# One-hots of a gate table with two tokens innermost in place of four, and the gate product as two instructions

## The chip, the cores and the metric

The kernel runs on one core of a Trainium2 chip. A core has a matrix engine (TensorE, PE in the profile, with the loading of its weights shown apart as PEld), three engines for elementwise work (VectorE or DVE, ScalarE or ACT, GpSimd or POOL), and a queue engine that here only starts transfers (SyncE or SP). They run their own instruction streams and wait for each other by semaphores. Operands lie in SBUF, matmul results in PSUM, in banks of 512 floats per partition. The metric is the device time of one execution in microseconds (us), the median of several. Before the change it is 2301.12 us, with three runs from 2299.87 to 2302.93.

## The reference

The reference is one layer of a decoder block over 256 tokens of width 2048: a combined projection, two kinds of attention, a merge with an output projection and a layer norm, then a PEER layer (a retrieval over 16,384 one-neuron experts) and a second layer norm. The change lies in the PEER layer, which computes, cut to its core:

```python
q = (yc @ w_q).reshape(PEER_CHUNK, PEER_HEADS, 2, half)
s1 = jnp.einsum('chd,nd->chn', q[:, :, 0], sub_k1)
s2 = jnp.einsum('chd,nd->chn', q[:, :, 1], sub_k2)
v1, i1 = lax.top_k(s1, PEER_TOPK)          # 16 of 128 keys, 8 heads
v2, i2 = lax.top_k(s2, PEER_TOPK)
...                                        # the best 16 of the 16 x 16 pairs
eid = jnp.take_along_axis(cid, j, axis=-1) # expert = 128 * key1 + key2
gate = jax.nn.softmax(sc, axis=-1)
act = jax.nn.gelu(jnp.einsum('chkd,cd->chk', u_tab[eid], yc))
return jnp.einsum('chk,chkd->cd', gate * act, v_tab[eid])
```

Each token thus has 8 x 16 = 128 slots, and a slot has a first key, a second key (both 0 to 127) and a gate.

## The kernel before

**The dense form.** Nothing is gathered. The kernel multiplies all 16,384 rows of u with the tokens (the U product), applies gelu, multiplies by a table G that holds for every expert and token the sum of the gates of that token's slots, and multiplies the result with all of v (the V product). u and v are streamed once from memory in pieces of 128 x 1024 floats.

**Exact products from two parts.** Each streamed piece `raw` is split into `hi` (a copy rounded by ScalarE, line 96) and `lo` (the rest, a subtraction on VectorE, line 97). A product of two such operands is three matmuls: hi with hi, hi with lo, lo with hi. All matmuls go through the helper `mm`, so most have line 189 in the profile, and they are told apart by their tiles. In the U product a matmul has 128 x 128 of u as weights and streams the 256 tokens of `yhi` or `ylo` into a bank `acc`.

**The gate table G.** For one token, G as a 128 x 128 table (first key by second key) is a sum over the token's 128 slots of one-hot(first key) times one-hot(second key) times gate. With the slots on the partitions that is one matmul. The transposed slots lie in `slotT`, 2-byte numbers, one row of 256 tokens per kind: first key, second key, and the gate in two parts (lines 1126 to 1128). For four tokens (a block q, 64 blocks in all) `g_onehot` makes on VectorE:

- `one`, the one-hots of both keys: a ramp `keys` of the 128 key numbers, each repeated for the four tokens, compared with the slots' keys (line 1189), 2 x 128 x 4 elements with the tokens innermost;
- `ob`, the one-hot of the second key times both parts of the gate (line 1190), again 2 x 128 x 4.

`g_mm` then takes for each of the four tokens the column k of `one` as weights and of `ob` as streamed operand, once for each part of the gate: 8 matmuls of 128 columns into a bank `lg`. The operands of one token are 128 elements of 2 bytes with a step of 4 elements. The deferred part of the block scales the four tables: part of the first half of G on VectorE, multiplied with gelu results already in G (line 1205), the rest on ScalarE (lines 1208, 1209).

**Order.** The order is the order of the code; there is no scheduler. `step` handles one streamed piece: it runs the deferred work, takes background work from a list `slots` as far as a credit goes (one credit a step; a block costs 1.05), splits the pieces for the next two steps (`W.ahead`, depth 2), issues the step's 24 U matmuls, and behind these the background work's matmuls. So in a step VectorE gets: line 1205 of the block whose matmuls ended the step before, then `one` and `ob` of a new block, then two subtractions of line 97 for the step after the next; and TensorE gets 24 U matmuls and the 8 matmuls of the block whose one-hots were made one step earlier. Every fourth step ScalarE also applies gelu to a finished bank (line 1241) and, while G is not ready, spills it to memory from its own queue (line 1245). `one` and `ob` have three buffers each, `lg` two banks. Transfers of u are started on SP (line 77) as soon as one of three `raw` buffers is free.

Of the kernel before, what the change touches and what calls it, by code (L numbers as in the profile page):

```python
# [11 lines left out]
F16 = mybir.dt.float16  # L12
# [3 lines left out]
AF = mybir.ActivationFunctionType  # L16
OP = mybir.AluOpType
# [4 lines left out]
S = 256  # L22
# [10 lines left out]
GSCALE = 2.0 ** 14  # L33
# [95 lines left out]
def block_kernel(ctx, tc, x, xT, w_in, rel_bias, onehot, lamq, lamk, subln_g, pe, w1, w2k, w2v, cmask,  # L129
                 wbda, wbnsa, wout, ln1_gT, ln1_bT, ln1_g, ln1_b, wq, subk, u, v, ln2_g, ln2_b, out):  # L130
    nc = tc.nc
    V, A, PE, GP = nc.vector, nc.scalar, nc.tensor, nc.gpsimd
# [52 lines left out]
    def bank(name, bufs):  # L185
        return ps.tile([128, 512], F32, name=name, bufs=bufs)

    def mm(o, a, b, start, stop):
        PE.matmul(o, a, b, start=start, stop=stop, skip_group_check=True)  # L189
# [679 lines left out]
    for q in range(2):  # L869
        for t in range(2):  # L870
            c = slice(HALF * q, HALF * q + HALF)
# [54 lines left out]
    yp = pY.enter_context(tc.tile_pool(name="yp", bufs=1, side="right"))  # L926
# [52 lines left out]
    pH.close()  # L979
    pX.close()  # L980
    pT = ExitStack()
    slotT = yp.tile([128, 4, S], F16, name="slotT")
    tk = pT.enter_context(tc.tile_pool(name="tk", bufs=1, side="right"))
    gb = lp.tile([128, 2, D], F32, name="gd")

# [33 lines left out]
    def h_rows():  # L1019
        for t in range(2):  # L1020
            for n in range(4):
                c = slice(n * 512, n * 512 + 512)
                d = r1[:, t, c]
                GP.tensor_tensor(d, d, gb[:, 0, c], op=OP.mult)
                GP.tensor_tensor(d, d, gb[:, 1, c], op=OP.add)
            GP.dma_start(h_d[:, t, :], r1[:, t, :])
# [92 lines left out]
    def sel_T(t):  # L1119
        tp = bank("tp", 1)  # L1120
        for c in range(3):
            PE.transpose(tp[:, 128 * c:128 * c + 128], sel[:, c, t, :], ident_k)

        def ev():
            ts = slice(128 * t, 128 * t + 128)
            A.copy(slotT[:, 0:2, ts], tp[:, 0:256].rearrange("p (c s) -> p c s", c=2))
            A.activation(slotT[:, 2, ts], tp[:, 256:384], AF.Copy, scale=GSCALE)
            V.scalar_tensor_tensor(slotT[:, 3, ts], tp[:, 256:384], GSCALE, slotT[:, 2, ts],
                                   op0=OP.mult, op1=OP.subtract)
        deferred.append(ev)  # L1130

    gs = {"done": False}
# [5 lines left out]
    def open_G(i):  # L1138
        if i == 0:
            h_rows()  # L1140
            pL.close()
        else:
            pT.close()
            gs["oh"] = pO.enter_context(tc.tile_pool(name="ohp", bufs=1, side="right"))
            gs["n0"] = len(stashed)
            keys = gs["keys"] = gs["oh"].tile([128, 128, 4], F16, name="keys")
            GP.iota(keys, pattern=[[1, 128], [0, 4]], base=0, channel_multiplier=0,
                    allow_small_or_imprecise_dtypes=True)
        gp = pG[i].enter_context(tc.tile_pool(name=f"gp{i}", bufs=1))
        gs["G", i] = gp.tile([128, HI, S], F32, name=f"G{i}")  # L1150

    bg(0.5, lambda: open_G(0))
    for c in range(2):
        if c == 0:
# [28 lines left out]

    def g_onehot(q):

        shape = [128, 2, 128, 4]
        one, ob = [gs["oh"].tile(shape, F16, name=x, bufs=3) for x in ("one", "ob")]
        key12, gate12 = [slotT[:, c:c + 2, None, 4 * q:4 * q + 4].to_broadcast(shape) for c in (0, 2)]
        V.tensor_tensor(one, gs["keys"][:, None, :, :].to_broadcast(shape), key12, op=OP.is_equal)
        V.tensor_tensor(ob, one[:, 1:2].to_broadcast(shape), gate12, op=OP.mult)  # L1190
        gs[q] = (one[:, 0], ob)

    def g_mm(q):
        gps = bank("lg", 2)
        oa, ob = gs.pop(q)
        for k in range(4):
            for c in range(2):
                mm(gps[:, 128 * k:128 * k + 128], oa[:, :, k], ob[:, c, :, k], k == 0 and c == 0, c == 1)

        def ev():  # L1200
            gv = gps.rearrange("p (t i) -> p i t", t=4)
            ts = slice(4 * q, 4 * q + 4)
            n0 = min(2 * gs["n0"], HI)
            g0, g1 = gs["G", 0], gs["G", 1]
            V.scalar_tensor_tensor(g0[:, 0:n0, ts], gv[:, 0:n0, :], 1.0 / GSCALE, g0[:, 0:n0, ts],
                                   op0=OP.mult, op1=OP.mult)
            if n0 < HI:
                A.activation(g0[:, n0:HI, ts], gv[:, n0:HI, :], AF.Copy, scale=1.0 / GSCALE)
            A.activation(g1[:, :, ts], gv[:, HI:I2, :], AF.Copy, scale=1.0 / GSCALE)
            if q == 63:  # L1210
                gs["done"] = True
                pO.close()
        deferred.append(ev)

    bg(0.1, lambda: open_G(1))
    for q in range(65):
        bg(GCOST, lambda q=q: g_onehot(q) if q < 64 else None, lambda q=q: g_mm(q - 1) if q else None)
# [270 lines left out]
```

## Time and profile before

| what | value |
|---|---|
| median of three runs | 2301.12 us |
| profiled execution, by the clock around it | 2305.7 us |
| its span, first to last instruction | 2303.9 us |
| TensorE busy | 2271.5 us (99%) |
| VectorE busy | 1436.8 us (62%) |
| ScalarE busy | 1116.7 us (48%) |
| stretch with the 64 gate blocks | 988.3 to 1236.1 us |
| granted TensorE clock, mean | 0.996 |

The busy shares are averages over the whole span. A timeline row gives the start, the time from the first start to the last end of a run of like instructions, the engine, the line, the operation with its tiles (output <- inputs), the shape, the count, and in brackets how long the engine sat idle before it and what ended that. Matmuls are pipelined: the time that one takes is longer than the time from its start to the next one's, and it is the second that counts. The pace of a run of n matmuls is its time less the length of one, over n - 1.

### The profile page before, as it was taken

What the parts mean: (1) busy time and instruction counts of PE and PEld (TensorE: products, weight loads), DVE (VectorE), ACT (ScalarE), POOL (GpSimd) and SP (SyncE); (2) the same over time, 40 slices, a digit from 0 to 9 for tenths busy, and PEclk for the clock granted to TensorE, in tenths of its full rate; (3) what the DMA queues carried; (4) which work ended last, traced back from release to release, by engine and by line L of the source; (5) the groups of instructions that cost most, each with busy time, mean ns of one, the idle gap of its engine ahead of it and who ended that gap; (6) DMA issues with size and microseconds to landing.
All of it is one profiled execution on the core that took longest, in us unless ns stands there. A gap on an engine that the chain in (4) does not pass through costs nothing.

```text
span 2303.9 us, 40869 instructions
## 1 busy us (share of the span) xinstructions
PE 2271.5 (99%) x15712; PEld 2084.5 (90%) x15712; DVE 1436.8 (62%) x2834; ACT 1116.7 (48%) x2153; POOL 245.8 (11%) x223
## 2 busy tenths in 40 slices
PE   9999999999999999999999999999999999999997
PEld 9989999999987999999999999998888888888786
DVE  5458664665657989977776555555555555555557
ACT  4455654665545544454444444444444444444443
POOL 1002234442002402200000000000000000000002
PEclk9999999999999999999999999999999999999999
DMA  7554564545575655554545666666666656667764
GB/s 241 185 182 150 177 188 138 156 143 174 184 234 174 221 181 173 181 173 158 159 157 174 184 187 188 187 188 198 190 187 188 189 187 190 185 191 234 243 210 145
DMA packets 119844, 424.73 MB, mean 184 GB/s; under 512 B 13876, under 2 KB 14212, under 8 KB 119392
## 3 DMA queue, kind: packets, MB, share of 16 engines
q1 hardware_dynamic: 111600, 398.90, 55.4%
q0 software_dynamic: 5600, 18.75, 2.7%
q10 hardware_dynamic: 2448, 4.46, 0.5%
q8 instruction: 123, 2.02, 0.3%
q14 instruction: 73, 0.60, 0.1%
HBM read 413.37 MB, written 8.69 MB: 183 GB/s over the span
## 4 chain that ended last, share of the span: by engine, by line
PE 86%; DVE 6%; DMA 4%; ACT 2%; issue 1%; POOL 0%; DVEq 0%; ACTq 0%; SPq 0%; POOLq 0%
PE acc L189 53%; PE o L189 27%; PE lg L189 4%; DVE lo L97 3%; DMA raw<-in_v_dram 2%; PE pv L189 1%; DMA raw<-in_wq_dram 1%; DMA raw<-in_wout_dram 1%; PE tp L527 1%; DMA raw<-in_w_in_dram 1%; ACT hi L96 1%; DVE eq L1095 0%; DVE st L890 0%; DVE r L922 0%; DVE eid L1099 0%
## 5 line engine op out<-in xcount | busy, mean ns | idle before, releaser
L97 DVE TENSOR_TENSOR lo<-raw,hi 128x512 fp32r<-128x512 f32 (+1 forms) x1422 | 969.4, 718 | 595.6 <-ACT hi L96 593.5
L96 ACT CAST hi<-raw 128x512 fp32r<-128x512 f32 (+1 forms) x1494 | 859.4, 615 | 730.0 <-PE o L189 317.5
L189 PE MATMUL acc<-yhi,hi 128*128 128x256 f32 x2112 | 597.6, 283 | 0.0
L189 PE MATMUL acc<-yhi,lo 128*128 128x256 f32 x2112 | 591.7, 280 | 3.8 <-DVE lo L97 3.7
L189 PE MATMUL acc<-ylo,hi 128*128 128x256 f32 x2112 | 589.4, 279 | 0.0
L189 PEld LDWEIGHTS acc<-yhi,lo 128*128 128x128 f32 x2112 | 396.6, 188 | 5.5 <-DVE lo L97 5.4
L189 PEld LDWEIGHTS acc<-ylo,hi 128*128 128x128 f32 x2112 | 397.4, 188 | 0.2
L189 PEld LDWEIGHTS acc<-yhi,hi 128*128 128x128 f32 x2112 | 396.8, 188 | 0.3
L189 PE MATMUL o<-hi,whi 128*128 128x512 f32 x1000 | 315.6, 396 | 1.3 <-ACT hi L96 0.8
L189 PE MATMUL o<-lo,whi 128*128 128x512 f32 x1000 | 316.3, 396 | 0.5
L189 PE MATMUL o<-hi,wlo 128*128 128x512 f32 x1000 | 314.6, 395 | 0.0
L189 PE MATMUL acc<-xhi,hi 128*128 128x256 f32 x1024 | 296.4, 289 | 2.9 <-ACT hi L96 2.9
L189 PE MATMUL acc<-xhi,lo 128*128 128x256 f32 x1024 | 292.0, 285 | 3.3 <-DVE lo L97 3.3
L189 PE MATMUL acc<-xlo,hi 128*128 128x256 f32 x1024 | 291.0, 284 | 0.0
L189 PEld LDWEIGHTS o<-hi,whi 128*128 128x128 f32 x1000 | 187.9, 188 | 48.3 <-ACT hi L96 2.3
L189 PEld LDWEIGHTS o<-lo,whi 128*128 128x128 f32 x1000 | 187.9, 188 | 47.8 <-DVE lo L97 2.8
L189 PEld LDWEIGHTS o<-hi,wlo 128*128 128x128 f32 x1000 | 188.0, 188 | 44.9
L189 PEld LDWEIGHTS acc<-xhi,lo 128*128 128x128 f32 x1024 | 197.6, 193 | 5.0 <-DVE lo L97 4.9
L189 PEld LDWEIGHTS acc<-xhi,hi 128*128 128x128 f32 x1024 | 197.7, 193 | 4.8 <-ACT hi L96 4.4
L189 PEld LDWEIGHTS acc<-xlo,hi 128*128 128x128 f32 x1024 | 197.7, 193 | 0.1
L1267 POOL DMA_DIRECT2D back<-act_d x17 | 9.2, 543 | 1234.5 <-DVE G L1275 626.8
L97 POOL TENSOR_TENSOR lo<-raw,hi 128x512 fp32r<-128x512 f32 x72 | 105.0, 1463 | 235.8 <-ACT hi L96 227.3
(308 smaller groups left out, 2215.5 us busy)
## 6 DMA issues: line engine op xcount, KB each, us to landing
raw<-in_u_dram SPq DMA_DIRECT2D x256, 512.0 KB, 3.9
raw<-in_v_dram SPq DMA_DIRECT2D x256, 512.0 KB, 4.3
raw<-in_w_in_dram SPq DMA_DIRECT2D x143, 512.0 KB, 3.8
raw<-in_wout_dram SPq DMA_DIRECT2D x32, 512.0 KB, 4.4
raw<-in_wbda_dram SPq DMA_DIRECT2D x16, 512.0 KB, 3.7
raw<-in_wbnsa_dram SPq DMA_DIRECT2D x16, 512.0 KB, 3.7
raw<-in_wq_dram SPq DMA_DIRECT2D x16, 512.0 KB, 3.9
raw<-in_w_in_dram SPq DMA_DIRECT2D x16, 280.0 KB, 2.9
```

Of the source, the lines that this page charges most:

```text
L96: self.nc.scalar.copy(hi[:, :w], r)
L97: (self.nc.gpsimd if self.share and b else sub).tensor_tensor(lo[:, :w], r, hi[:, :w].bitcast(F32), op=OP.subtract)
L189: PE.matmul(o, a, b, start=start, stop=stop, skip_group_check=True)
L527: PE.transpose(tp[:, 128 * b:128 * b + 128], P[:, 128 * b:128 * b + 128], ident)
L1267: GP.dma_start(t, act_d[vorder[n]])
```

## The change

The tokens of a block are laid out as two pairs, with the two tokens of a pair innermost. `one` and `ob` get the shape 4 x 128 x 2, and from key to key of one token there are 2 elements (4 bytes) in place of 4 (8 bytes). So that the compared keys of a block can be read in that form, `slotT` becomes block by kind by token. The key ramp repeats each number twice in place of four times. The product with the gate, one instruction of 1,024 elements before, becomes two of 512, one for each part of the gate. Lines move by up to two.

```diff
@@ -979,7 +979,7 @@
     pH.close()
     pX.close()
     pT = ExitStack()
-    slotT = yp.tile([128, 4, S], F16, name="slotT")
+    slotT = yp.tile([128, S // 4, 4, 4], F16, name="slotT")
     tk = pT.enter_context(tc.tile_pool(name="tk", bufs=1, side="right"))
     gb = lp.tile([128, 2, D], F32, name="gd")
 
@@ -1122,10 +1122,11 @@
             PE.transpose(tp[:, 128 * c:128 * c + 128], sel[:, c, t, :], ident_k)
 
         def ev():
-            ts = slice(128 * t, 128 * t + 128)
-            A.copy(slotT[:, 0:2, ts], tp[:, 0:256].rearrange("p (c s) -> p c s", c=2))
-            A.activation(slotT[:, 2, ts], tp[:, 256:384], AF.Copy, scale=GSCALE)
-            V.scalar_tensor_tensor(slotT[:, 3, ts], tp[:, 256:384], GSCALE, slotT[:, 2, ts],
+            qs_ = slice(32 * t, 32 * t + 32)
+            keys_, gate_ = [tp[:, a:b].rearrange("p (c q s) -> p q c s", q=32, s=4) for a, b in ((0, 256), (256, 384))]
+            A.copy(slotT[:, qs_, 0:2, :], keys_)
+            A.activation(slotT[:, qs_, 2:3, :], gate_, AF.Copy, scale=GSCALE)
+            V.scalar_tensor_tensor(slotT[:, qs_, 3:4, :], gate_, GSCALE, slotT[:, qs_, 2:3, :],
                                    op0=OP.mult, op1=OP.subtract)
         deferred.append(ev)
 
@@ -1143,8 +1144,8 @@
             pT.close()
             gs["oh"] = pO.enter_context(tc.tile_pool(name="ohp", bufs=1, side="right"))
             gs["n0"] = len(stashed)
-            keys = gs["keys"] = gs["oh"].tile([128, 128, 4], F16, name="keys")
-            GP.iota(keys, pattern=[[1, 128], [0, 4]], base=0, channel_multiplier=0,
+            keys = gs["keys"] = gs["oh"].tile([128, 128, 2], F16, name="keys")
+            GP.iota(keys, pattern=[[1, 128], [0, 2]], base=0, channel_multiplier=0,
                     allow_small_or_imprecise_dtypes=True)
         gp = pG[i].enter_context(tc.tile_pool(name=f"gp{i}", bufs=1))
         gs["G", i] = gp.tile([128, HI, S], F32, name=f"G{i}")
@@ -1183,19 +1184,20 @@
 
     def g_onehot(q):
 
-        shape = [128, 2, 128, 4]
-        one, ob = [gs["oh"].tile(shape, F16, name=x, bufs=3) for x in ("one", "ob")]
-        key12, gate12 = [slotT[:, c:c + 2, None, 4 * q:4 * q + 4].to_broadcast(shape) for c in (0, 2)]
-        V.tensor_tensor(one, gs["keys"][:, None, :, :].to_broadcast(shape), key12, op=OP.is_equal)
-        V.tensor_tensor(ob, one[:, 1:2].to_broadcast(shape), gate12, op=OP.mult)
-        gs[q] = (one[:, 0], ob)
+        one, ob = [gs["oh"].tile([128, 4, 128, 2], F16, name=x, bufs=3) for x in ("one", "ob")]
+        key12, gate12 = [slotT[:, q, c:c + 2, :].rearrange("p c (a b) -> p (c a) b", b=2)[:, :, None, :]
+                         .to_broadcast([128, 4, 128, 2]) for c in (0, 2)]
+        V.tensor_tensor(one, gs["keys"][:, None, :, :].to_broadcast([128, 4, 128, 2]), key12, op=OP.is_equal)
+        for c in range(2):
+            V.tensor_tensor(ob[:, 2 * c:2 * c + 2], one[:, 2:4], gate12[:, 2 * c:2 * c + 2], op=OP.mult)
+        gs[q] = (one, ob)
 
     def g_mm(q):
         gps = bank("lg", 2)
         oa, ob = gs.pop(q)
         for k in range(4):
             for c in range(2):
-                mm(gps[:, 128 * k:128 * k + 128], oa[:, :, k], ob[:, c, :, k], k == 0 and c == 0, c == 1)
+                mm(gps[:, 128 * k:128 * k + 128], oa[:, k // 2, :, k % 2], ob[:, 2 * c + k // 2, :, k % 2], k == 0 and c == 0, c == 1)
 
         def ev():
             gv = gps.rearrange("p (t i) -> p i t", t=4)
```

On VectorE, inside the stretch of the gate blocks, two steps follow each other like this before the change (`one` and `ob` are the one-hots and the product of a block, `lo` the subtractions of the streamed pieces, `lg` a bank of finished gate matmuls, `G` the table):

```order
L1189 TENSOR_TENSOR one<-keys,slotT 128x1024
L1190 TENSOR_TENSOR ob<-one,slotT 128x1024
L97 TENSOR_TENSOR lo<-raw,hi 128x512 x2
L1205 SCALAR_TENSOR_TENSOR G_9650<-lg,G_9650 128x34x4
L1189 TENSOR_TENSOR one<-keys,slotT 128x1024
L1190 TENSOR_TENSOR ob<-one,slotT 128x1024
```

And at the same place after it:

```order
L1190 TENSOR_TENSOR one<-keys,slotT 128x1024
L1192 TENSOR_TENSOR ob<-one,slotT 128x512 x2
L97 TENSOR_TENSOR lo<-raw,hi 128x512 x2
L1207 SCALAR_TENSOR_TENSOR G_9650<-lg,G_9650 128x34x4
L1190 TENSOR_TENSOR one<-keys,slotT 128x1024
L1192 TENSOR_TENSOR ob<-one,slotT 128x512 x2
```

Nothing changes its place; the one product is two instructions of half the size.

On TensorE a gate block stands between U matmuls like this before the change (the load of the weights `one` is a row of its own, and the waits of an instruction stand in brackets):

```order
L189 MATMUL acc<-yhi,lo 128x256
L189 LDWEIGHTS one [waits PE_49,DVE_49]
L189 MATMUL lg<-ob,one 128x128 [waits Activation_49]
L189 LDWEIGHTS one
L189 MATMUL lg<-ob,one 128x128
L189 LDWEIGHTS one
L189 MATMUL lg<-ob,one 128x128
```

And after it:

```order
L189 MATMUL acc<-yhi,lo 128x256
L189 LDWEIGHTS one [waits PE_49,DVE_49]
L189 MATMUL lg<-ob,one 128x128 [waits Activation_49]
L189 LDWEIGHTS one
L189 MATMUL lg<-ob,one 128x128 [waits DVE_49]
L189 LDWEIGHTS one
L189 MATMUL lg<-ob,one 128x128
```

The order is the same; the second matmul of the block, the first that reads the second product, has a wait for VectorE of its own.

## Rows read from the trace of the kernel before

**Rows 1.** The page: busy time by engine, and its chain of waits by line.
```profile
PE 2271.5 (99%) x15712; PEld 2084.5 (90%) x15712; DVE 1436.8 (62%) x2834; ACT 1116.7 (48%) x2153; POOL 245.8 (11%) x223
...
PE acc L189 53%; PE o L189 27%; PE lg L189 4%; DVE lo L97 3%; DMA raw<-in_v_dram 2%; PE pv L189 1%; DMA raw<-in_wq_dram 1%; DMA raw<-in_wout_dram 1%; PE tp L527 1%; DMA raw<-in_w_in_dram 1%; ACT hi L96 1%; DVE eq L1095 0%; DVE st L890 0%; DVE r L922 0%; DVE eid L1099 0%
```

**Rows 2.** Busy time by stretch: us, each engine (count), TensorE clock, DMA share, GB/s.
```profile
988.30:1236.10 247.80, 247.80 (x2100) 244.44 (x2099) 182.88 (x324) 114.37 (x277) 0.00 (x0) 1.00 0.50 160
1236.10:1300.00 63.90, 63.90 (x545) 63.90 (x544) 33.69 (x52) 30.58 (x55) 0.00 (x0) 1.00 0.61 189
```

**Rows 3.** The chain of waits inside the stretch, in time: start, us, what.
```profile
1051.88 0.95 PE lg L189 x8
1052.83 2.83 PE acc L189 x24
```

**Rows 4.** Groups of 1000 to 1220 us: count, busy us, mean ns, idle before.
```profile
L189 PE MATMUL lg<-ob,one 128*128 128x128 f16 x449 | 62.6, 296 | 0.0
...
L97 DVE TENSOR_TENSOR lo<-raw,hi 128x512 fp32r<-128x512 f32 x118 | 76.1, 686 | 14.2 <-ACT hi L96 14.2
...
L1190 DVE TENSOR_TENSOR ob<-one,slotT 128x1024 f16<-128x1024 f16 x57 | 39.4, 692 | 2.0
L1189 DVE TENSOR_TENSOR one<-keys,slotT 128x1024 f16<-128x1024 f16 x57 | 38.8, 682 | 0.0
```

**Rows 5.** Timeline of TensorE around one gate block.
```profile
1051.72 1.11 PE L189 MATMUL lg<-ob,one 128*128 128x128 f16 x8
1052.58 0.37 PE L189 MATMUL acc<-yhi,hi 128*128 128x256 f32 x1
1052.79 0.28 PE L189 MATMUL acc<-ylo,hi 128*128 128x256 f32 x1
```

**Rows 6.** Timeline of TensorE around 15 two-byte matmuls of the attention.
```profile
440.28 0.60 PE L189 MATMUL pv<-vd,wt 128*128 128x64 bf16 x15
440.71 0.36 PE L189 MATMUL acc<-xhi,hi 128*128 128x256 f32 x1
440.92 0.28 PE L189 MATMUL acc<-xlo,hi 128*128 128x256 f32 x1
```

**Rows 7.** By tile (one, wt): ns min/median/max, first and last start, forms.
```profile
L189 PEld LDWEIGHTS <-one x512: 112/117/136, 991.2 to 1235.7; 128*128 128x128 f16 x171
...
L189 PE MATMUL pv<-vd,wt x528: 192/193/276, 210.2 to 531.8; 128*128 128x64 bf16 x160, 128*128 128x128 f32 x16
L189 PEld LDWEIGHTS <-wt x480: 95/98/100, 407.7 to 531.8; 128*128 128x128 f16 x160
```

**Rows 8.** Timeline of the weight loads, the first two of a gate block.
```profile
1051.72 0.15 PEld L189 LDWEIGHTS <-one 128*128 128x128 f16 x2
```

**Rows 9.** By tile (kcT) and timeline: matmuls with 4-byte weights, 32 columns streamed.
```profile
L189 PE MATMUL lg<-kcT,r x32: 194/276/277, 351.7 to 355.0; 128*128 128x32 f32 x32
...
351.65 3.66 PE L189 MATMUL lg<-kcT,r 128*128 128x32 f32 x32
```

**Rows 10.** Timeline of VectorE over one step of the stretch.
```profile
1060.43 0.30 DVE L1205 SCALAR_TENSOR_TENSOR G<-lg,G 128x136 f32<-128x136 f32 x1 [0.95 <-PE lg L189]
1060.65 0.68 DVE L1189 TENSOR_TENSOR one<-keys,slotT 128x1024 f16<-128x1024 f16 x1
1061.36 0.69 DVE L1190 TENSOR_TENSOR ob<-one,slotT 128x1024 f16<-128x1024 f16 x1
1061.97 1.29 DVE L97 TENSOR_TENSOR lo<-raw,hi 128x512 fp32r<-128x512 f32 x2
1064.21 0.30 DVE L1205 SCALAR_TENSOR_TENSOR G<-lg,G 128x136 f32<-128x136 f32 x1 [0.95 <-PE lg L189]
```

**Rows 11.** The same for a step in which ScalarE also evacuates and spills.
```profile
1228.62 0.30 DVE L1205 SCALAR_TENSOR_TENSOR G<-lg,G 128x136 f32<-128x136 f32 x1 [0.95 <-PE lg L189]
...
1231.04 1.29 DVE L97 TENSOR_TENSOR lo<-raw,hi 128x512 fp32r<-128x512 f32 x2 [0.80 <-ACT hi L96]
1232.40 0.30 DVE L1205 SCALAR_TENSOR_TENSOR G<-lg,G 128x136 f32<-128x136 f32 x1
```

## The prediction, made before the changed kernel was run

> **What bounds the kernel now.** I read four views in this order. First the page's busy shares and its chain of waits: TensorE is busy 99% of the span, and the chain is made of its matmuls, with little else [rows 1]. So a microsecond off TensorE's stream is a microsecond off the end, and a microsecond more on another engine costs nothing until that engine makes TensorE wait. Next the stretch table around the changed code: while the gate table is built TensorE is busy for all of 247.8 us, VectorE for 182.9 us, ScalarE for 114.4 us, at a granted clock of 1.00 (the upper of its two levels), and in the 64 us behind it, where the same stream runs without the gate table, TensorE is again busy throughout, with 189 GB/s in place of 160 [rows 2]. The chain inside the stretch alternates between 24 matmuls of the U product, 2.83 us, and 8 matmuls of the gate table, 0.95 us [rows 3]: a step is 3.78 us, and there are 64 such blocks. So the question is what the 512 gate matmuls cost on TensorE, and whether VectorE, with a step of its own inside those 3.78 us, still keeps up.
>
> The reader is to see something odd in the 0.95 us. Eight gate matmuls start to end take 1.11 us, one lasts 0.296 us [rows 4, 5], so they start (1.11 - 0.296)/7 = 0.116 us apart. That is the pace of the U matmuls around them (2.83/24 = 0.118 us), which stream twice as many columns: 256 against 128. A second family of 2-byte matmuls, in the attention, streams 64 columns that lie side by side: 15 of them in 0.60 us, one 0.193 us [rows 6, 7], so 0.029 us apart, or 0.058 us for 128 columns. The gate matmuls thus take twice the time of their column count. What they share with the U matmuls is the bytes spanned per partition: 128 columns at 8 bytes from key to key span 1,024 bytes, and 256 columns of 4 bytes side by side span 1,024 bytes. The stepped read is the candidate.
>
> **The change part by part.**
>
> Step between keys, 8 to 4 bytes. A gate matmul now spans 512 bytes. By the span, with U as the yardstick, it takes half of 0.118 = 0.059 us; by the columns, with the attention as the yardstick, 0.058 us. Both rows give the same floor, and the other bound is 0.116 us, no gain, if it is not the span that counts but the fact of a step. I take 0.058, since the span explains three shapes at once (gate, U, attention) and the fact of a step explains only one.
>
> Not all eight intervals shrink. Behind the last gate matmul comes a U matmul whose 4-byte weights have to be loaded beside it. After the attention's short matmuls that load shows: the first U matmul there is followed by the next after 0.21 us in place of 0.118 [rows 6], and where 4-byte loads alone set the pace (32 columns streamed per load) matmuls come (3.66 - 0.276)/31 = 0.109 us apart [rows 9], one of them lasting 0.276 us. So the last interval stays near 0.116 and seven shrink: 7 x 0.058 = 0.41 us a block, 64 x 0.41 = 26.0 us. If the last one shrinks too it is 29.7 us.
>
> Second wait on TensorE. The order shows that the second matmul of a block now waits for VectorE too. Its product is made a step before it is used, so the semaphore is long there. All that the start and end of a block cost now, one such wait included, is 0.95 - 8 x 0.116 = 0.02 us [rows 3, 5]. Bounds: nothing, or one interval of 0.058. I take 0.02: 64 x 0.02 = 1.3 us back.
>
> Two products in place of one, on VectorE. From start to start a VectorE instruction of 136 elements takes 0.22 us (1060.43 to 1060.65) and the product of 1,024 two-byte elements 0.61 us (1061.36 to 1061.97) [rows 10]. A two-byte instruction of 1,024 elements lasts 682 to 692 ns, a four-byte one of 512 lasts 686 [rows 4], so two-byte elements go in pairs: 512 paces. The line through 136 and 512 paces has 1.04 ns a pace and 0.08 us fixed. A half product is 0.08 + 256 x 1.04 ns = 0.35 us, two are 0.69: 0.08 us more a step, 5 us over 64 steps. What covers them: VectorE sits idle 0.95 us a step waiting for the gate matmuls [rows 10]. The step shrinks to about 3.39 us, so of the 0.95 there remain 0.95 - 0.39 - 0.08 = 0.48 us. Cost: nothing.
>
> The thin place is one step in four, where ScalarE also evacuates and spills the gelu result. There the step of VectorE is 3.78 us with no idle time before its last instruction, 1228.62 to 1232.40, 0.80 us of it waiting for ScalarE [rows 11]. The longer product hides in those 0.80 us. With TensorE at 3.39 us this step ends 0.39 us late; behind it on VectorE stand the next one-hots (needed a step later) and the two splits of U (for the step after the next). The three following steps have 0.48 us each to catch up, so TensorE should not feel it. If the cover were gone, 16 such steps at 0.39 us would give back 6 us.
>
> The rest. The table of the transposed keys is written in another layout by two small evacuations, twice in the kernel; the key ramp halves in size. TensorE streams U meanwhile. Nothing, a microsecond at worst. Transfers: the step asks for the same bytes in 10% less time, 160 to 178 GB/s, and the stretch behind runs at 189 without stopping TensorE [rows 2]. Nothing.
>
> Sum: 26.0 - 1.3 = 24.7 us. The profiled execution took 2305.7 us by the clock around it (its span 2303.9), so it would come to 2281.0; the median of the runs shown is 2301.1, 4.6 lower, so I forecast 2276.4, that is 2276. The likeliest case's own range is 2270 (eight intervals and a little more) to 2282 (a pace of 0.062, a wait of 0.06).
>
> **The rivals.**
>
> *A step is a step.* If stepped two-byte columns go at half pace however near they lie, TensorE's stream is unchanged and VectorE's 0.08 us vanish in its 0.95 us: 2301. For it: 0.116 us is also what half pace would give against 0.058, and no row shows another step. Against it: the U matmuls, 4 bytes from column to column, make 256 columns in the same 0.118 us, so elements 4 bytes apart can be fetched at that pace. [...]
>
> *The loads bind next.* The gate's weights are stepped as well: their load lasts 117 ns, the attention's contiguous one 98 [rows 7]. Were a load to hold its successor for its whole length, the pace could fall only from 0.116 to about 0.098: 64 x 7 x 0.018 = 8 us, 2293. For it: 117 ns is almost the interval. Against it: the attention's loads of 98 ns follow each other every 0.029 us, and the first two gate loads of a block together end 0.15 us after the first began [rows 8], which two holds of 0.117 could not.
>
> *VectorE binds.* The rows of two elements could make VectorE take one element a pace. One one-hot instruction is then 0.08 + 1024 x 1.04 ns = 1.14 us in place of 0.61, two half products 1.22 in place of 0.61: 1.14 us more a step on top of 3.78 - 0.95 = 2.83, so 3.97. From 3.78 on it decides, since the splits of U then come late: 64 x 0.19 = 12 us slower, 2313, whatever TensorE gains. For it: no row has pairs as innermost run. Against it: runs of four, with repeats between them, go in pairs now [rows 4], and two elements fill a pair. [...]
>
> **How the numbers follow.** The forecast has 0.62, the loads 0.12, no gain 0.18, VectorE 0.08. Something over 0.2% (4.6 us) can be told from no change here: faster 0.74, same 0.18, slower 0.08. A range from 2269 to 2303 takes in the first three and leaves out VectorE and the tails.
>
> **What would show it.** The gate matmuls should start about 0.058 us apart, eight taking some 0.70 us from first start to last end; the block on the chain should fall from 0.95 to 0.55 to 0.57 us, a step to about 3.39; the stretch that was 247.8 us should be some 223; VectorE's idle time before the multiplication of the gate result should fall to half a microsecond or less; and outside the stretch nothing should move. The pace still at 0.116 says the step itself costs; near 0.1, with loads as long as intervals, says the loads; one-hots of over a microsecond say VectorE. Gate matmuls at 0.058 with TensorE idle in the stretch would mean that I misjudged the step of VectorE and ScalarE.

## The result, and the profile after

The changed kernel takes 2275.21 us (median of 4 runs, 2273.62 to 2277.22) against 2301.32 us before: a ratio of 0.9887, 95% interval 0.987 to 0.9904. The profiled execution took 2277.2 us against 2305.7, its span 2275.4 against 2303.9.

The stretch with the 64 gate blocks, by engine (columns as in [rows 2]), and the stretch behind it:

```profile
985.00:1208.20 223.20, 223.20 (x2123) 220.35 (x2122) 187.20 (x391) 115.58 (x281) 1.43 (x1) 1.00 0.58 181
1208.20:1270.00 61.80, 61.80 (x527) 61.80 (x526) 32.40 (x49) 28.91 (x51) 0.00 (x0) 1.00 0.63 189
```

TensorE is still busy without a gap, so its stream got shorter and no new wait took the place. The two windows do not begin alike: this one begins 5.0 us before the first gate matmul, that of [rows 2] 2.9 us. From the first block to the last, start to start, it is 217.1 us in place of 243.8. VectorE is now busy for 187 of 223 us where it was for 183 of 248 [rows 2]. The chain of waits inside the stretch, beside [rows 3]:

```profile
1040.51 0.47 PE lg L189 x8
1040.98 2.88 PE acc L189 x24
```

The eight gate matmuls fell from 0.95 to 0.47 us; the 24 U matmuls behind them rose from 2.83 to 2.88. The likely reason is the load of their first 4-byte weights, which lasts 0.188 us beside matmuls that are now 0.057 us apart; no run takes that load away by itself. A step from block to block is 3.357 us in place of 3.780. TensorE's timeline around one block answers to [rows 5]:

```profile
1050.42 0.63 PE L189 MATMUL lg<-ob,one 128*128 128x128 f16 x8
1050.86 0.36 PE L189 MATMUL acc<-yhi,hi 128*128 128x256 f32 x1
1051.06 0.28 PE L189 MATMUL acc<-ylo,hi 128*128 128x256 f32 x1
```

And the instructions on the tile `one` to [rows 4, 7] (ns min/median/max, first and last start):

```profile
L189 PEld LDWEIGHTS <-one x512: 96/97/101, 990.0 to 1207.5; 128*128 128x128 f16 x171
L189 PE MATMUL lg<-ob,one x512: 218/218/233, 990.0 to 1207.5; 128*128 128x128 f16 x171
L1192 DVE TENSOR_TENSOR ob<-one,slotT x128: 415/422/428, 987.2 to 1202.4; 128x512 f16<-128x512 f16 x128
L1190 DVE TENSOR_TENSOR one<-keys,slotT x64: 678/681/692, 986.5 to 1201.3; 128x1024 f16<-128x1024 f16 x64
```

Inside a block the matmuls now start 0.057 us apart (median; 0.118 before, both read start by start from the two traces), and one lasts 0.218 us in place of 0.296. The load fell from 117 to 97 ns, as long as the attention's contiguous one (98 [rows 7]). The one-hot instruction kept its 681 ns for 1,024 two-byte elements, against 685 for 512 four-byte ones on line 97, so runs of two elements still go in pairs. VectorE over three steps, the first of them one in which ScalarE also evacuates and spills, beside [rows 10, 11]:

```profile
1054.44 0.30 DVE L1207 SCALAR_TENSOR_TENSOR G<-lg,G 128x136 f32<-128x136 f32 x1 [0.46 <-PE lg L189]
...
1056.86 1.29 DVE L97 TENSOR_TENSOR lo<-raw,hi 128x512 fp32r<-128x512 f32 x2 [0.73 <-ACT hi L96]
1058.07 0.29 DVE L1207 SCALAR_TENSOR_TENSOR G<-lg,G 128x136 f32<-128x136 f32 x1
...
1059.00 0.76 DVE L1192 TENSOR_TENSOR ob<-one,slotT 128x512 f16<-128x512 f16 x2
1059.67 1.29 DVE L97 TENSOR_TENSOR lo<-raw,hi 128x512 fp32r<-128x512 f32 x2
1061.16 0.30 DVE L1207 SCALAR_TENSOR_TENSOR G<-lg,G 128x136 f32<-128x136 f32 x1 [0.20 <-PE lg L189]
```

Read the brackets on line 1207: 0.46 us of waiting for TensorE in a settled step (0.95 before), none behind the step that ScalarE holds, 0.20 in the one after. VectorE comes late there and catches up within two steps.

### The profile page after: what moved, and what is told of

It is laid out like the page before. It is cut to its first block, busy times and chain, and to the rows that moved or that the text cites. A ratio compares the mean times of both kernels' runs of the same rounds, so it can differ in the third digit from the quotient of the medians.

```text
span 2275.4 us, 40934 instructions
## 1 busy us (share of the span) xinstructions
PE 2244.3 (99%) x15712; PEld 2058.5 (90%) x15712; DVE 1439.0 (63%) x2898; ACT 1116.3 (49%) x2153; POOL 246.1 (11%) x223
## 4 chain that ended last, share of the span: by engine, by line
PE 86%; DVE 7%; DMA 4%; ACT 2%; issue 1%; POOL 0%; SPq 0%; DVEq 0%; ACTq 0%; POOLq 0%
PE acc L189 53%; PE o L189 28%; DVE lo L97 3%; PE lg L189 3%; DMA raw<-in_v_dram 2%; PE pv L189 1%; DMA raw<-in_w_in_dram 1%; DMA raw<-in_wout_dram 1%; PE tp L527 1%; DMA raw<-in_wq_dram 1%; ACT hi L96 1%; DVE eq L1095 0%; DVE st L890 0%; DVE r L922 0%; DVE eid L1099 0%
```

## The experiments

**Which of the two stepped operands counts.** The first kernel keeps the streamed operand of the change and gives the weights back their 8 bytes; the second does the reverse. The lines that make `one` and `ob` in these shapes are left out here; both kernels keep two products of 512.

```diff
-                mm(..., oa[:, k // 2, :, k % 2], ob[:, 2 * c + k // 2, :, k % 2], ...)
+                mm(..., oa[:, 0, :, k], ob[:, 2 * c + k // 2, :, k % 2], ...)    # first: one is 2 x 128 x 4
+                mm(..., oa[:, k // 2, :, k % 2], ob[:, c, :, k], ...)            # second: ob is 2 x 128 x 4
```

> The streamed operand lies at 4 bytes from key to key as after the change, the weights stay at 8 bytes as before it. Theory (the bytes that the streamed operand spans set the pace): gate matmuls 0.057 us apart, the load of the weights still 117 ns long, time near 2275 us. Rival (the stepped weights set the pace): 0.116 us apart, near 2302 us. Rival (each of the two slows it by itself): between 0.08 and 0.116 us, 2285 to 2302 us.

> The mirror image: weights at 4 bytes from key to key, the streamed operand at 8 bytes. Theory (span of the streamed operand): gate matmuls 0.116 us apart, loads of 97 ns, time near 2302 us. Rival (weights): 0.057 us apart, near 2275 us. Rival (each by itself): as the other kernel, above 2285 us in both.

The first: 2278.4 us, ratio 0.9897 (0.9881 to 0.9914). By tile, and on the chain:

```profile
L189 PEld LDWEIGHTS <-one x512: 111/113/138, 988.6 to 1208.1; 128*128 128x128 f16 x171
L189 PE MATMUL lg<-ob,one x512: 218/221/253, 988.6 to 1208.2; 128*128 128x128 f16 x171
```
```profile
1032.74 0.51 PE lg L189 x8
1033.25 2.88 PE acc L189 x24
```

The second: 2301.1 us, ratio 0.9998 (0.9988 to 1.0007):

```profile
L189 PEld LDWEIGHTS <-one x512: 96/115/119, 989.3 to 1232.7; 128*128 128x128 f16 x171
L189 PE MATMUL lg<-ob,one x512: 276/296/300, 989.3 to 1232.8; 128*128 128x128 f16 x171
```
```profile
1030.83 0.94 PE lg L189 x8
1031.76 2.83 PE acc L189 x24
```

Nearly the whole gain hangs on the streamed operand: 0.059 us apart (median) with weights at 8 bytes, 0.116 with the stream at 8 bytes. Weights at 8 bytes cost 0.03 us a step (3.39 against 3.357). Both one-sided forms keep the two product instructions, and the second is no slower than before, so those cost nothing there. One expectation failed: the loads of the second kernel were to last 97 ns and last 115, though its weights lie at 4 bytes. So the 117 ns of the kernel before do not tell of stepped weights alone; a slow stream beside a load lengthens its record too (115 ns with the stream at 8 bytes, 97 with it at 4, the weights at 4 bytes in both).

**What in the step counts.** In the next three kernels the step itself changes after every 8 blocks. They read `one` and `ob`, or a constant, as one flat run, so what they build is not the table G; only what the reading costs is of use. The first two:

```diff
+        fa, fb = [x.rearrange("p c n k -> p (c n k)") for x in gs.pop(q)]    # one and ob, flat
+        s = q // 8 + 1
...
-                mm(..., oa[:, :, k], ob[:, c, :, k], ...)
+                o = (2 * k + c) % s
+                mm(..., fa[:, 128 * k:128 * k + 128], fb[:, o:o + 127 * s + 1:s], ...)   # streamed operand
+                mm(..., fa[:, o:o + 127 * s + 1:s], fb[:, 128 * k:128 * k + 128], ...)   # weights
```

> Kernel before, but the 64 gate blocks stream their operand with a step of 1, 2, 3 ... 8 elements of 2 bytes (8 blocks each, in this order), and weights side by side; the gate table so read is not the right one. Theory (span, 0.115 us per 1,024 bytes, not under the 0.057 of the columns): 0.057, 0.057, 0.086, 0.115, 0.144, 0.172, 0.201, 0.230 us apart. Rival (a step above two elements halves the pace, whatever its size): 0.057, 0.057, then 0.115 six times. [...]

The timeline of TensorE, one block of eight matmuls for each of the steps 1 to 8:

```profile
997.31 0.62 PE L189 MATMUL lg<-ob,one 128*128 128x128 f16 x8
...
1024.08 0.64 PE L189 MATMUL lg<-ob,one 128*128 128x128 f16 x8
...
1051.35 0.86 PE L189 MATMUL lg<-ob,one 128*128 128x128 f16 x8
...
1083.01 1.09 PE L189 MATMUL lg<-ob,one 128*128 128x128 f16 x8
...
1117.48 1.31 PE L189 MATMUL lg<-ob,one 128*128 128x128 f16 x8
...
1149.97 1.54 PE L189 MATMUL lg<-ob,one 128*128 128x128 f16 x8
...
1182.69 1.76 PE L189 MATMUL lg<-ob,one 128*128 128x128 f16 x8
...
1223.19 1.98 PE L189 MATMUL lg<-ob,one 128*128 128x128 f16 x8
```

Median start to start: 0.056, 0.058, 0.084, 0.116, 0.143, 0.173, 0.200, 0.227 us. The expectation from bytes spanned meets every one within 0.003 us. A step that halves the pace whatever its size meets step 4 and misses steps 3 and 5 to 8. Only how TensorE reads its operands differs here from the kernel before, so VectorE's instructions have no part in it. The load records of these side-by-side weights last 98 ns at step 1 and 115 to 117 from step 4 on, as in the second kernel above. This kernel took 2311.6 us in its one run.

> The same with the roles swapped: the streamed operand side by side, the weights at a step of 1 to 8 elements, 8 blocks each; the gate table so read is not the right one. Theory (the streamed operand sets the pace): 0.057 us apart at every step up to 4, the load growing from 97 ns by about 5 to 10 ns an element of step, and the pace giving way only where the load needs more than 0.057 us to follow its predecessor. Rival (weights set it): 0.057, 0.057, 0.086, 0.115 and on as the span grows.

Rows of the same kind for the weights at steps 1, 3, 5, 7 and 8, the streamed operand side by side:

```profile
990.04 0.62 PE L189 MATMUL lg<-ob,one 128*128 128x128 f16 x8
...
1046.93 0.63 PE L189 MATMUL lg<-ob,one 128*128 128x128 f16 x8
...
1099.92 0.64 PE L189 MATMUL lg<-ob,one 128*128 128x128 f16 x8
...
1160.06 0.66 PE L189 MATMUL lg<-ob,one 128*128 128x128 f16 x8
...
1190.65 0.71 PE L189 MATMUL lg<-ob,one 128*128 128x128 f16 x8
```

Matmuls start 0.056 us apart (median) at every step up to 7, while the median load grows from 98 to 132 ns, and 0.062 at step 8, with 148 ns. A load thus lies beside the matmul of its predecessor, stepped or not, and sets the pace only at the very end of this range. The exception is the first interval of a block, which grows from 0.066 us at step 1 to 0.103 at step 7; that is the 0.04 us by which the step from block to block grows, from 3.342 to 3.380. 2273.3 us in its one run.

> Kernel before, but the gate blocks stream from a constant tile with a step of 8, 9, 10, 11, 12, 13, 14 and 16 elements of 2 bytes (8 blocks each), weights side by side; the gate table so read is not the right one. Theory (bytes spanned): 0.227, 0.255, 0.284, 0.312, 0.340, 0.37, 0.40, 0.45 us apart, growing all the way. Rival (whole lines of 16 bytes are fetched, each once): 0.227 at step 8, where every element has a line of its own, and no more from there on.

Here the product goes to one buffer and the stream comes from a constant tile `big` of 2,048 elements. Blocks at step 8, 12 and 16:

```profile
994.81 1.98 PE L189 MATMUL lg<-big,one 128*128 128x128 f16 x8
...
1146.72 1.98 PE L189 MATMUL lg<-big,one 128*128 128x128 f16 x8
...
1261.64 2.02 PE L189 MATMUL lg<-big,one 128*128 128x128 f16 x8
```

My theory falls in its letter and the rival stands: 0.227 us at step 8, 0.227 at 12, 0.232 at 16, and 0.237 at most in the median (step 11). From the point on where each element has 16 bytes to itself, spreading them further costs at most 0.010 us, where bytes spanned would have doubled the price; why some steps lie those few ns higher is not shown. What fits the medians of both kernels is the number of 16-byte lines that the stream touches: 64 lines in 0.116 us, 96 in 0.173, 128 in 0.227 to 0.237, so about 1.8 ns a line, until the 128 columns themselves need 0.056. Below step 8 lines and bytes are the same count, which is why bytes predicted so well. (2344.6 us, one run.)

**How much cover VectorE has left.** A spare instruction on VectorE behind the products, of 512 and of 1,024 elements:

```diff
+        spare = gs["oh"].tile([128, 2, 128, 2], F16, name="spare", bufs=1)   # half; in the whole, 4 in place of 2
+        V.tensor_tensor(spare, gs["keys"][:, None, :, :].to_broadcast([128, 2, 128, 2]), key12[:, 0:2], op=OP.is_equal)
```

> The changed kernel with one spare VectorE instruction of 512 two-byte elements a block (0.35 us from start to start). Theory (VectorE has 0.46 us to spare in three steps of four, the fourth is held by ScalarE at 3.63): a mean step of (3 x 3.25 + 3.63)/4 = 3.34, still under TensorE's 3.357, so no change, 2274 to 2277 us. Rival (VectorE already makes TensorE late after the change): 0.35 x 64 = 22 us slower, or a good part of it.

> The same with a spare instruction of 1,024 elements (0.61 us). Theory: a normal step of VectorE becomes 3.51 us, the mean (3 x 3.51 + 3.63)/4 = 3.54, over TensorE's 3.357: 64 x 0.18 = 12 us slower less what the splits lead by, 2283 to 2287 us, and TensorE waits for the splits. Rival (VectorE is hidden whatever it does here): no change, 2275 us.

The half: 2273.5 us, ratio 0.9873 (0.9857 to 0.989), TensorE's step 3.357 throughout. VectorE's wait for the gate matmuls is all but gone (us in total, times, longest, between 985 and 1240 us; the changed kernel, then this one, in which gaps of 0.07 and 0.12 us remain that the list leaves out):

```profile
DVE G L1207 <- PE lg L189: 17.5, 45, 0.9
...
DVE G L1209 <- PE lg L189: 1.3, 3, 0.5
```

The whole: 2280.2 us, ratio 0.9889 (0.986 to 0.9919), which the time alone cannot tell from no change. The trace can. From the first gate block to the last, start to start, TensorE needs 220.9 us in place of 217.1, and now waits for the splits:

```profile
PEld acc L189 <- DVE lo L97: 2.6, 10, 0.5
...
PE acc L189 <- DVE lo L97: 0.6, 2, 0.3
```

Two steps of VectorE there, the first of them held by ScalarE:

```profile
1099.83 0.29 DVE L1209 SCALAR_TENSOR_TENSOR G<-lg,G 128x136 f32<-128x136 f32 x1
...
1101.43 0.69 DVE L1194 TENSOR_TENSOR spare<-keys,slotT 128x1024 f16<-128x1024 f16 x1
1102.24 1.29 DVE L97 TENSOR_TENSOR lo<-raw,hi 128x512 fp32r<-128x512 f32 x2
1103.45 0.29 DVE L1209 SCALAR_TENSOR_TENSOR G<-lg,G 128x136 f32<-128x136 f32 x1
...
1106.87 0.29 DVE L1209 SCALAR_TENSOR_TENSOR G<-lg,G 128x136 f32<-128x136 f32 x1
```

The direction was as expected, the size was not: 3.8 us on the trace for the 8 to 12 forecast. A normal step without waiting lasts mostly 3.41 us, not 3.51, so VectorE's own work in the changed kernel is 3.41 - 0.61 = 2.80 us. I had counted 3.357 - 0.46 = 2.90; the other 0.1 us is there only when VectorE waits, and what it consists of is not shown. The mean is (3 x 3.41 + 3.62)/4 = 3.46, 0.11 over TensorE. The splits lead by about a step, and the two steps without a block in between give some of it back, so TensorE slows only after the first 20 blocks, and later after about ten.

**The second wait.** In a block, the matmul that reads the later product comes first, so that only it waits.

```diff
-            for c in range(2):
-                mm(..., k == 0 and c == 0, c == 1)
+            for c in (1, 0):
+                mm(..., k == 0 and c == 1, c == 0)
```

> The changed kernel with the two matmuls of each token in the other order, so that the first matmul of a block waits for the later product and the second needs no wait. Theory of the prediction (the second wait costs 0.02 us a block): a step of 3.337 in place of 3.357 us, 1.3 us in all. Rival (a semaphore that stands long before costs nothing): 3.357 us.

The step is 3.357 us with one wait as with two, the first interval of a block is 0.071 us in both, and the chain reads alike (2275.8 us, one run):

```profile
1041.05 0.47 PE lg L189 x8
1041.52 2.88 PE acc L189 x24
```

The rival holds; the second wait costs nothing that this trace resolves.

**The ends of a block.** Two blocks are issued together every second step, beside the changed kernel on the same chip:

```diff
-        bg(GCOST, ..., lambda q=q: g_mm(q - 1) if q else None)
+        bg(GCOST, ..., (lambda q=q: g_two(q)) if q and q % 2 == 0 else None)
+    # g_two(q) is g_mm(q - 2), then g_mm(q - 1)
```

> The changed kernel with the matmuls of two gate blocks issued together every second step. Theory (what a block costs beyond its columns is its start, 73 against 57 ns, and the load of the next 4-byte weights, 229 against 57 + 118 ns: 0.07 us a block): two steps take 2 x 3.357 - 0.07 = 6.64 us, 32 x 0.07 = 2.2 us less in all, about 2273 us, which may be too little to tell by time; the trace tells it by the step. Rival (VectorE or the two banks, now both waited for at once, make TensorE late): two steps above 6.72 us and a time above that of the changed kernel.

> The changed kernel once more, on the chip of the run beside it: 2275 us, 0.989 of before, 3.357 us a step.

```profile
1044.14 0.93 PE lg L189 x16
1045.07 5.71 PE acc L189 x48
```

Two steps take 6.64 us, as expected. By time it is 2271.4 us, ratio 0.9867 (0.985 to 0.9884), and the changed kernel beside it 2274.2 us, 0.988 (0.9861 to 0.9898): lower by about what the trace says, but the intervals overlap. The trace shows the gain; the time does not separate it.

## Why the prediction was right, step by step

- **The pace at 4 bytes.** Forecast 0.058 us, measured 0.057. The span was the right choice, and the mirror kernels and the steps 1 to 8 show it. The ground given for it was thinner than it reads: the U and the attention matmuls fit their column counts as well as their spans (256 columns at the attention's pace are 0.116 us, measured 0.118), so only the gate matmuls asked for a span, and they alone could not tell it from a step that halves the pace. Its wording was too wide: lines of 16 bytes count, not bytes, as the steps beyond 8 show (0.227 to 0.237 us, where bytes would have asked for up to 0.45). At the two steps of the change both say the same. Eight matmuls took 0.63 us and not the 0.70 of the signs, since the forecast kept the length of one at 0.296.
- **Seven intervals, not eight.** The seven inside a block add up to 0.415 us, 0.816 before: 0.40 less, where 0.41 was forecast. The 0.118 that the median fell from is a little above my 0.116 because the first interval of a block is shorter, 0.106 us; after the change the first is the longer one, 0.071, so the block gains little at its start. The last matmul of a block and the U matmul behind it together took 0.256 us before and 0.229 after (start of the one to start of the next but one). Less 0.118 for the U matmul, the last interval is 0.111, close to the forecast 0.116; but before it was 0.138 and not 0.116, so it did shrink, by 0.027. That term was put at nothing and is worth 1.7 us. The chain shows a block as 0.47 us, under the 0.55 to 0.57 of the signs, because it books the rest of that last interval with the U matmuls, 0.05 us more.
- **The second wait.** Forecast 0.02 us a block, measured nothing, 1.3 us. The 0.02 that were read as the start and the end of a block lie in that last interval of 0.138.
- **Two products on VectorE.** Forecast 0.69 us from the first to the splits in place of 0.61, measured 0.67 (1059.00 to 1059.67). Hidden, as forecast: TensorE lost nothing, and a further 0.35 us would have been hidden too.
- **The step that ScalarE holds.** I read 3.78 us as its work; it needs 3.63 (1054.44 to 1058.07). From its start to the splits it is 2.42 us in both traces; from the splits to the line that ends it, 1.36 us before [rows 11] and 1.21 after. So 0.15 us of the 3.78 was waiting, with no bracket to show it. It comes 0.27 late, not 0.39.
- **The sum.** A step of 3.39 was forecast, 3.357 measured: 64 x 0.423 = 27.1 us in place of 24.7. The wait and the last interval are 3.0 us of the difference, and the seven intervals and the U matmuls beside the block take 0.6 back. The profiled executions differ by 28.5 us, the medians by 26.1. Of the 28.5, 26.7 lie between the first and the last block's start, 1.2 before the first block and 0.6 behind the last one's start. The 1.2 cannot be put down to the change: in the other kernels here, the first block starts anywhere from 986.7 to 993.8 us. That 2276 came within a microsecond of the median is in part luck, since the sum was 2.4 us short on the trace.
- **The rivals.** "A step is a step" falls with the change itself, 0.057 us at a step of two elements, and with steps 3 (0.084) and 5 to 8 (0.143 to 0.227). Against its columns (0.056 us, step 1) the matmul takes twice the time at step 4 and 1.5 times at step 3, and only at step 2, at 0.058, is it nearly free. "The loads bind next" falls with the weights at steps up to 7, 0.056 us apart beside loads of up to 132 ns; the 117 ns that stood for it are reached by side-by-side weights too, beside a slow stream. "VectorE binds" falls with the one-hots at 681 ns; runs of two do go in pairs.

## What to carry to other kernels

Compare the pace of a matmul, start to start, with that of another of known layout in the same trace; a two-byte stream that takes twice the time of its columns may be read too sparsely (here 0.118 us at a step of 4 elements, 0.057 at 2), and the layout that VectorE writes can mend it as long as VectorE has idle time in that very step (here 0.95 us of it, 0.46 after the change). Count the 16-byte lines that the streamed operand touches, at about 1.8 ns each here, against 0.056 us per 128 columns. Weights could be stepped further here: at a step of 7 elements a block of eight lost 0.04 us in all.

## What the runs showed of the hardware that was not expected

The stream's price levels off: 128 two-byte columns take 0.227 us at a step of 8 elements and 0.232 at 16. Loads of stepped weights grow from 98 to 132 ns (steps 1 to 7) without moving the 0.056 us between matmuls, other than the first interval of a block. And a wait whose semaphore has stood for a step costs TensorE nothing that a trace resolves: 3.357 us a step with it and without it.
